# Differential attention's keys and queries prepared for both maps in one 128-row pass, with copies inside SBUF that put the halves in place

## The chip, the cores and the metric

The kernel runs on one core of one Trainium2 chip. The metric is the device time of one execution in microseconds. TensorE (PE) multiplies matrices, VectorE (DVE), ScalarE (ACT) and GpSimd (POOL) work elementwise on 128 rows (partitions) at a time, and SyncE (SP) issues all the DMAs of this kernel, one after the other in its queue. Each engine takes its instructions in a fixed order.

## The reference

One streaming-encoder layer over 1024 prompt tokens and 32 sample tokens. The part that matters here is head group B, differential attention: four heads, two softmax maps each, 64 features a map.

```python
dq = proj[..., o3:o4].reshape(b, s, H_B, 2, D_HB)     # 4 heads, 2 maps, 64 features
dk = proj[..., o4:o5].reshape(b, s, H_B, 2, D_HB)
...
s = jnp.einsum('bqhmd,bkhmd->bhmqk', qb, k).astype(jnp.float32) * scale
s = s - slopes[None, :, None, None, None] * dist      # and a block-causal mask
p = jax.nn.softmax(s, axis=-1)
w = jnp.einsum('bhmqk,hm->bhqk', p, coef32)           # map 0 minus lambda times map 1
return jnp.einsum('bhqk,bkhd->bqhd', w, v)
```

The layer goes on with latent attention (eight heads), an output projection, a layer norm, a gated convolution network, a second norm and a gate.

## The kernel before

All tensors are f32, and a product of two of them is made from a high part (rounded to fp32r) and a low part (the rest), in three matmuls: high by high, high by low, low by high. The stages follow each other: projections of the input, differential attention, latent attention (from about 387 us), output projection, feed-forward network, gate.

`dk` and `dq` hold, for each differential head h, a tile `hd(dk, h)` of 128 rows: rows 0 to 63 are map 0's features, rows 64 to 127 map 1's. A score product has only 64 features, so the kernel stacks parts on the 128 rows of PE: a tile K with the high part of the keys in one half of its rows and their low part in the other, and two tiles Qh and Ql with the queries' high and low part repeated in both halves. Then one matmul with Qh and one with Ql (L554 and L555) make a score block with all its parts.

`prep_b(h)` makes K, Qh and Ql. It is a list of six steps, and map m has three of them: `keys(m)` rounds the map's 64 rows of keys (ACT, L484) and of queries (POOL, L119 by way of L485), `low(m, 0)` and `low(m, 512)` subtract the high part from the 64 rows, 512 columns at a time (POOL, L82), and the last issues one DMA (L495) that copies the queries' 64 rows, high and low, to the other half. The keys' low part is written straight into the other half by POOL. So a head takes, on POOL, two roundings of 64x1024 and eight subtractions of 64x512, on ACT two roundings of 64x1024, and two DMAs of 512 KB.

`UnitB(h, i)` is one block of 128 queries, i from 7 (1024 keys) down to 0 (128 keys). `front` makes the scores of each map into a PSUM tile `pd` (two of these exist), a softmax pass on DVE with the bias and the row's maximum (L524), an exponential on ACT (L558), then on DVE a reciprocal, a coefficient and the combination of the two maps (L562). `back` transposes the result (PE L571, ACT L572), `values` multiplies by the values (PE L582), and after every four blocks POOL takes a power (L589), DVE scales the rows (four L592), and PE transposes them (L599). Head 0's steps of `prep_b` run between the products that make the differential values (`tok_tile` with `out_dv`, three matmuls at L144 to L146 for each of eight parts) and the sample tokens' attention (`sb_...`, with the transposes L424 and the products L438 and L442, which hold one `pd` tile, and with the key rows that `dk_rows` copies on ACT at L359 and writes out at L360). The steps for head h+1 are hooked to the blocks of head h.

The order of each engine's instructions isn't the order in which the code is written: a scheduler with a timeline of its own sets it at build time, by when it takes the operands to be there. `paced` and `held` tell it what an instruction shall not come ahead of; they add no wait on the chip.

## Time and profile before

| | |
|---|---|
| median of three runs | 1571.83 us (1571.09 to 1573.90) |
| the profiled execution | 1573.72 us, of it 1571.6 us from its first to its last instruction |
| granted TensorE clock, mean | 0.99 of full speed |
| PE busy | 1502.3 us, 96% |
| DVE busy | 965.8 us, 61% |
| ACT busy | 714.3 us, 45% |
| POOL busy | 342.6 us, 22% |

Busy time is the time in which an engine had an instruction in hand. The shares are means over all stages; what a change is worth is read in its own stage, here from 195 to 387 us.

### The profile page before, as it was taken

The numbers are of one execution on the slowest core, as the hardware profiler recorded it, in microseconds if no ns is written. First come the engines' busy times: TensorE is split into PE (matmuls) and PEld (weight loads), VectorE is DVE, ScalarE is ACT, GpSimd is POOL, SyncE is SP. The second block draws the span as 40 slices with busy tenths as digits, with TensorE's granted clock in tenths as the row PEclk, the third lists the DMA queues.
The fourth block names the chain that finished last, engine by engine and source line by source line (L and its number), as shares of the span: only waits on it lengthen the run. The fifth ranks groups of instructions, "written<-read, shape, count | busy, mean of one in ns | idle before, by whom it ended". The sixth has DMA issues, their size and how long they took to land.

```text
span 1571.6 us, 25325 instructions
## 1 busy us (share of the span) xinstructions
PE 1502.3 (96%) x9787; PEld 1361.5 (87%) x9787; DVE 965.8 (61%) x1944; ACT 714.3 (45%) x1754; POOL 342.6 (22%) x394
## 2 busy tenths in 40 slices
PE   7999998888989999989999999999989999998998
PEld 7999987768878789879999999999978787876887
DVE  4113336785767757598677777777788524279332
ACT  4223346777777765056455555555552302122111
POOL 0002034542454320001001111111120000049311
PEclk9999999999999999999999999999999999999999
DMA  6113251121110215132222222222265524130111
GB/s 208 48 48 89 71 168 48 28 69 37 25 49 15 65 48 202 41 101 56 74 82 82 82 82 68 69 72 81 88 225 164 160 50 123 68 113 28 41 44 44
DMA packets 125868, 127.89 MB, mean 81 GB/s; under 512 B 14701, under 2 KB 105461, under 8 KB 125493
## 3 DMA queue, kind: packets, MB, share of 16 engines
q1 hardware_dynamic: 125749, 126.28, 26.4%
q8 instruction: 77, 1.26, 0.3%
q14 instruction: 42, 0.34, 0.1%
HBM read 93.83 MB, written 26.07 MB: 76 GB/s over the span
## 4 chain that ended last, share of the span: by engine, by line
PE 80%; DVE 9%; ACT 6%; DMA 2%; issue 2%; POOL 1%; SPq 0%; DVEq 0%; ACTq 0%; POOLq 0%
PE pm L144 13%; PE pm L146 13%; PE pm L145 13%; PE pd L1227 5%; PE pd L1225 5%; PE pd L1226 5%; PE pm L1225 4%; PE pm L1227 4%; PE pm L1226 4%; DVE h L82 3%; ACT h L85 2%; PE pm L822 2%; DVE h L524 1%; PE pm L152 1%; PE pm L153 1%
## 5 line engine op out<-in xcount | busy, mean ns | idle before, releaser
L144 PE MATMUL pm<-h,h 128*128 128x512 f32 (+4 forms) x1076 | 366.8, 341 | 6.9 <-DVE h L82 3.4
L146 PE MATMUL pm<-h,h 128*128 128x512 f32 (+4 forms) x1076 | 363.2, 338 | 0.5 <-DVE h L82 0.5
L145 PE MATMUL pm<-h,h 128*128 128x512 f32 (+4 forms) x1076 | 362.9, 337 | 0.0
L144 PEld LDWEIGHTS pm<-h,h 128*128 128x128 f32 x1076 | 204.5, 190 | 28.9 <-DVE h L82 4.2
L146 PEld LDWEIGHTS pm<-h,h 128*128 128x128 f32 x1076 | 203.3, 189 | 20.0 <-DVE h L82 0.9
L145 PEld LDWEIGHTS pm<-h,h 128*128 128x128 f32 x1076 | 203.5, 189 | 19.1 <-issue 0.5
L85 ACT CAST h<-t 128x1024 fp32r<-128x1024 f32 (+6 forms) x91 | 82.0, 912 | 211.3 <-PE pm L146 94.3
L82 DVE TENSOR_TENSOR h<-t,h 128x1024 fp32r<-128x1024 f32 (+6 forms) x81 | 88.9, 1107 | 100.4 <-ACT h L85 100.3
L82 DVE TENSOR_TENSOR h<-pm,h 128x256 fp32r<-128x256 f32 (+7 forms) x221 | 101.8, 485 | 47.5 <-ACT h L85 45.4
L1238 DVE SCALAR_TENSOR_TENSOR h<-h,cp,h 128x1058 f32<-128x1058 f32 x88 | 115.8, 1318 | 21.5 <-ACT h L1246 20.7
L1212 ACT COPY h<-pd 128x256 f32<-128x256 f32 (+1 forms) x258 | 56.2, 270 | 124.5 <-PE pd L1227 124.4
L85 ACT CAST h<-pm 128x256 fp32r<-128x256 f32 (+7 forms) x221 | 88.2, 426 | 44.2 <-PE pm L803 19.6
L1225 PE MATMUL pm<-h,s 128*128 128x264 f32 x360 | 102.5, 287 | 4.6 <-ACT h L1212 4.6
L82 DVE TENSOR_TENSOR h<-h,h 128x512 fp32r<-128x512 f32 (+4 forms) x166 | 101.0, 640 | 2.1 <-ACT h L85 2.1
L1226 PE MATMUL pm<-h,s 128*128 128x264 f32 x360 | 101.8, 285 | 0.0
L1227 PE MATMUL pm<-h,s 128*128 128x264 f32 x360 | 99.9, 286 | 0.0
L1227 PE MATMUL pd<-h,s 128*128 128x264 f32 x344 | 98.0, 285 | 0.0
L1225 PE MATMUL pd<-h,s 128*128 128x264 f32 x344 | 97.8, 284 | 0.0
L1226 PE MATMUL pd<-h,s 128*128 128x264 f32 x344 | 97.7, 284 | 0.0
L1387 DVE TENSOR_TENSOR h<-pm,h 128x512 f32<-128x512 f32 x48 | 32.9, 684 | 75.4 <-PE pm L146 75.4
L82 DVE TENSOR_TENSOR s<-h,s 128x512 fp32r<-128x512 f32 (+1 forms) x96 | 60.5, 642 | 29.3 <-ACT s L85 29.1
L178 POOL TENSOR_TENSOR sm<-sm,neghalf 128x1 f32<-128x1 f32 (+1 forms) x37 | 22.7, 614 | 253.9 <-DVE sm L177 249.0
(326 smaller groups left out, 3733.6 us busy)
## 6 DMA issues: line engine op xcount, KB each, us to landing
h<-in_w_up SPq DMA_DIRECT2D x44, 512.0 KB, 5.0
zd<-h SPq DMA_DIRECT2D x22, 529.0 KB, 4.1
t<-zd SPq DMA_DIRECT2D x24, 384.0 KB, 3.6
t<-in_w_down SPq DMA_DIRECT2D x16, 512.0 KB, 3.2
h<-in_x_p SPq DMA_DIRECT2D x15, 512.0 KB, 5.7
t<-in_w_in SPq DMA_DIRECT2D x14, 512.0 KB, 4.0
h<-h SPq DMA_DIRECT2D x8, 512.0 KB, 5.0
t<-in_w_o SPq DMA_DIRECT2D x8, 512.0 KB, 3.5
```

The lines of the kernel that those rows point to most:

```text
L82: return eng.tensor_tensor(out, x, y, ALU.subtract)
L85: c = ACT.copy(hi, src)
L144: PE.matmul(ps, sh, mh, start=(i == 0), stop=False)
L145: PE.matmul(ps, sh, ml, start=False, stop=False)
L146: PE.matmul(ps, sl, mh, start=False, stop=(i == last))
L822: PE.matmul(po[:, c : c + 256], vt[k // 4][:, k % 4, h % 4], pts[k // 4][:, hl, k % 4], start=(k == 0 and hl == 0), stop=(k == kt - 1 and ...
L1212: ACT.copy(x, y)
L1225: PE.matmul(ps[:, :BW], w[:, 0, k], c[:, k, 0], start=first and k == 0, stop=False, skip_group_check=True)
L1226: PE.matmul(ps[:, :BW], w[:, 0, k], c[:, k, 1], start=False, stop=False, skip_group_check=True)
L1227: PE.matmul(ps[:, :BW], w[:, 1, k], c[:, k, 0], start=False, stop=k == 3, skip_group_check=True)
L1238: DVE.scalar_tensor_tensor(z[:, j], U[:, j, i : i + T], cp[:, i, m + j * NF : m + j * NF + 1], z[:, j], ALU.mult, ALU.add)
L1387: DVE.tensor_tensor(d, ps[:n], d, ALU.add)
```

## The change

The six steps of `prep_b` become five. `begin` takes all three tile pairs at once (K for both maps, q0 and q1) and rounds all 128 rows of keys (one ACT instruction) and of queries (one POOL instruction) into map 0's tiles. `low_k` subtracts on 128 rows, two instructions of 512 columns, into the tile that will be map 1's Qh (t), and issues three DMAs of 256 KB: map 1's high keys to map 1's K, and the two halves of t to where map 1's and map 0's low keys belong. `low_q` subtracts on 128 rows, two instructions, and issues three DMAs of 512 KB: map 1's queries from q0's rows 64 to 127 into both halves of q1, and map 0's queries from q0's rows 0 to 63 over q0's rows 64 to 127. The last writes where the two ahead of it read, and these write where the keys' DMAs read.

```diff
@@ -475,26 +475,35 @@
                 load(bm[0][:, :1024], a["c_dist"])
             paced(scale(POOL, bm[h][:, :1024], bm[max(h - 1, 0)][:, :1024], 0.25 if h else -2.0))
 
-        def keys(m):
-            r, q = m * 64, 64 - m * 64
-            if m == 0:
-                V["k"] = pair()
-            K, Q = V["k"][:, m], pair()
-            Qh, Ql = Q[:, 0], Q[:, 1]
-            paced(ACT.copy(K[r : r + 64, :1024], hd(dk, h)[r : r + 64, :1024]))
-            paced(scale(POOL, Qh[r : r + 64, :1024], hd(dq, h)[r : r + 64, :1024], 1.0))
-            kq[h, m] = (K, Qh, Ql, Q)
-
-        def low(m, c):
-            r, q = m * 64, 64 - m * 64
-            K, Qh, Ql, Q = kq[h, m]
+        def begin():
+
+            V["k"], q0, q1 = pair(), pair(), pair()
+            K = V["k"]
+            kq[h, 0], kq[h, 1] = (K[:, 0], q0[:, 0], q0[:, 1], q0), (K[:, 1], q1[:, 0], q1[:, 1], q1)
+            paced(ACT.copy(K[:, 0, :1024], hd(dk, h)[:, :1024]))
+            paced(scale(POOL, q0[:, 0, :1024], hd(dq, h)[:, :1024], 1.0))
+
+        def low_k(c):
+            K, t = kq[h, 0][0], kq[h, 1][1]
             cs = slice(c, c + 512)
-            paced(sub(POOL, Ql[r : r + 64, cs], hd(dq, h)[r : r + 64, cs], f(Qh[r : r + 64, cs])))
-            paced(sub(POOL, K[q : q + 64, cs], hd(dk, h)[r : r + 64, cs], f(K[r : r + 64, cs])))
+            paced(sub(POOL, t[:, cs], hd(dk, h)[:, cs], f(K[:, cs])))
             if c:
-                SP.dma_start(f(Q[q : q + 64, :, :1024]), f(Q[r : r + 64, :, :1024]))
-
-        return [lambda: (bias(), keys(0)), lambda: low(0, 0), lambda: low(0, 512), lambda: keys(1), lambda: low(1, 0), lambda: low(1, 512)]
+
+                K1 = kq[h, 1][0]
+                SP.dma_start(f(K1[64:128, :1024]), f(K[64:128, :1024]))
+                SP.dma_start(f(K1[0:64, :1024]), f(t[64:128, :1024]))
+                SP.dma_start(f(K[64:128, :1024]), f(t[0:64, :1024]))
+
+        def low_q(c):
+            q0, q1 = kq[h, 0][3], kq[h, 1][3]
+            cs = slice(c, c + 512)
+            paced(sub(POOL, q0[:, 1, cs], hd(dq, h)[:, cs], f(q0[:, 0, cs])))
+            if c:
+                SP.dma_start(f(q1[0:64, :, :1024]), f(q0[64:128, :, :1024]))
+                SP.dma_start(f(q1[64:128, :, :1024]), f(q0[64:128, :, :1024]))
+                SP.dma_start(f(q0[64:128, :, :1024]), f(q0[0:64, :, :1024]))
+
+        return [lambda: (bias(), begin()), lambda: low_k(0), lambda: low_k(512), lambda: low_q(0), lambda: low_q(512)]
 
     steps += prep_b(0)
```

The scheduler moves instructions in answer. Lines behind the change stand nine lines further down in the new file (L563 and L564 are L554 and L555, L580 is L571, L591 is L582, L608 is L599, L519 is L510). First PE, from the sample tokens' products to the first differential scores; `pd_2284` is the sample tokens' accumulator, `pd_2445` and `pd_2452` the scores of head 0's first block (maps 0 and 1) before. The difference:

```order
 L424 MATMUL pm_2264<-ident,s_2095 128x128
 L438 MATMUL pd_2284<-t_2285,s_1650 128x512
-L554 MATMUL pd_2445<-h_2358,h_2359 128x512
-L555 MATMUL pd_2445<-h_2358,h_2359 128x512
-L554 MATMUL pd_2445<-h_2358,h_2359 128x512
-L555 MATMUL pd_2445<-h_2358,h_2359 128x512
 L424 MATMUL pm_2268<-ident,s_2095 128x128
 L438 MATMUL pd_2284<-t_2285,s_1650 128x512
```

And where they stand in the changed kernel, as `pd_2443` and `pd_2450`, behind all the products of the differential values:

```order
L146 MATMUL pm_2395<-h_2005,h_89 128x256
L442 MATMUL pd_2284<-rows_s,ptl 128x512
L563 MATMUL pd_2443<-h_2358,h_2359 128x512
L564 MATMUL pd_2443<-h_2358,h_2359 128x512
L563 MATMUL pd_2443<-h_2358,h_2359 128x512
L564 MATMUL pd_2443<-h_2358,h_2359 128x512
L563 MATMUL pd_2450<-h_2358,h_2360 128x512
```

Both maps' scores of the first block have gone from ahead of the four products of the values to behind them; before, the second block's scores stood at that place.

The second place is PE where head 0 ends. Before, `pd_2710` and `pd_2717` are head 1's first scores:

```order
L571 MATMUL pm_2702<-ident,h_2609 128x128 x3
L554 MATMUL pd_2710<-h_2464,h_2465 128x512
L555 MATMUL pd_2710<-h_2464,h_2465 128x512
L554 MATMUL pd_2710<-h_2464,h_2465 128x512
L555 MATMUL pd_2710<-h_2464,h_2465 128x512
L582 MATMUL pm_2695<-h_1597,s_2701 128x128 x3
L554 MATMUL pd_2717<-h_2464,h_2569 128x512
```

In the changed kernel they are `pd_2706` and `pd_2713`:

```order
L580 MATMUL pm_2698<-ident,h_2608 128x128 x3
L608 MATMUL pm_2734<-ident,sm_2664 128x128
L591 MATMUL pm_2691<-h_1597,s_2697 128x128 x3
L580 MATMUL pm_2760<-ident,h_2640 128x128 x2
L608 MATMUL pm_2734<-ident,sm_2664 128x128 x3
L580 MATMUL pm_2788<-ident,h_2676 128x128
L563 MATMUL pd_2706<-h_2462,h_2463 128x512
```

Head 1's first scores now stand behind head 0's last transposes, its last block (L580 of `h_2676`) among them; the same holds where heads 1 and 2 meet.

The third place is SP's queue during head 0's preparation. `h_2358` is K, `h_2359` q0, `h_2360` q1 (first t):

```order
L360 DMA out_dk_p<-sm_2132 128x512
L494 DMA h_2358<-h_2360 64x1024
L495 DMA h_2358<-h_2360 64x1024
L519 DMA out_dv_p<-h_1597 128x512
L503 DMA h_2360<-h_2359 64x2x1024
L360 DMA out_dk_p<-sm_2167 128x512
L360 DMA out_dk_p<-sm_2175 128x512
L502 DMA h_2360<-h_2359 64x2x1024
L519 DMA out_dv_p<-h_1597 128x512
L360 DMA out_dk_p<-sm_2210 128x512
L360 DMA out_dk_s<-sm_2218 32x512
L504 DMA h_2359<-h_2359 64x2x1024
```

Between the same writes of key rows (L360) there was one copy (L495) before; now there are five, of which L503, L502 and L504 wait for copies ahead of them.

## Rows read from the trace of the kernel before

**Rows 1.** The page of the profile: the span, the busy time of PE, and the chain that ended last by engine.

```profile
span 1571.6 us, 25325 instructions
...
PE 1502.3 (96%) x9787; PEld 1361.5 (87%) x9787; DVE 965.8 (61%) x1944; ACT 714.3 (45%) x1754; POOL 342.6 (22%) x394
...
PE 80%; DVE 9%; ACT 6%; DMA 2%; issue 2%; POOL 1%; SPq 0%; DVEq 0%; ACTq 0%; POOLq 0%
```

**Rows 2.** Busy time by stretch. Columns: the stretch, its length, then each engine's busy us (instructions), the granted clock as a share of full speed, the DMA engines' share and GB/s.

```profile
core 0: us, PE busy (x) PEld busy (x) DVE busy (x) ACT busy (x) POOL busy (x), PEclk, DMA share, GB/s
223.00:244.00 21.00, 21.00 (x126) 16.24 (x125) 5.29 (x13) 5.97 (x14) 1.04 (x1) 1.00 0.30 103
244.00:265.80 21.80, 19.73 (x135) 16.78 (x134) 17.45 (x51) 18.16 (x54) 12.53 (x12) 1.00 0.26 61
265.80:292.60 26.80, 23.72 (x156) 20.66 (x154) 22.34 (x63) 21.75 (x60) 14.46 (x11) 0.94 0.10 21
292.60:325.60 33.00, 27.30 (x181) 23.79 (x181) 26.34 (x74) 24.31 (x72) 18.23 (x15) 0.95 0.27 60
325.60:350.00 24.40, 18.00 (x99) 13.82 (x98) 22.89 (x59) 19.34 (x52) 6.94 (x5) 0.92 0.21 52
350.00:387.00 37.00, 33.09 (x214) 30.02 (x213) 23.74 (x78) 25.87 (x87) 10.88 (x11) 0.91 0.16 40
387.00:860.00 473.00, 448.29 (x3177) 415.52 (x3176) 345.90 (x795) 275.87 (x701) 108.66 (x163) 0.99 0.23 70
```

**Rows 3.** Timeline of DVE, the first block of head 0 (128x1024) and the second (128x896). Columns: start us, duration us, engine, line, operation, tiles, shapes, count, and in brackets the idle time before it with what ended it.

```profile
228.83 1.22 DVE L524 CUSTOM_DVE_ANT_0 h<-pd,s 128x1024 f32<-128x1024 f32 x1 [0.49 <-PE pd L555]
...
231.88 1.28 DVE L562 SCALAR_TENSOR_TENSOR h<-h,sm 128x1024 f32<-128x1024 f32 x1
...
245.68 1.09 DVE L524 CUSTOM_DVE_ANT_0 h<-pd,s 128x896 f32<-128x896 f32 x1 [12.51 <-PE pd L555]
...
247.36 1.09 DVE L524 CUSTOM_DVE_ANT_0 h<-pd,s 128x896 f32<-128x896 f32 x1 [0.52 <-PE pd L555]
```

**Rows 4.** Timeline of PE, the score matmuls of the first block: the first and the last of map 0's four and of map 1's four.

```profile
223.34 0.80 PE L554 MATMUL pd<-h,h 128*128 128x512 f32 x1
...
224.44 0.39 PE L555 MATMUL pd<-h,h 128*128 128x512 f32 x1
...
227.61 0.48 PE L554 MATMUL pd<-h,h 128*128 128x512 f32 x1
...
228.40 0.40 PE L555 MATMUL pd<-h,h 128*128 128x512 f32 x1
```

**Rows 5.** The chain that ended last, in order of time, from 211 us: start us, duration us, what.

```profile
211.05 4.09 DMA out_dk_p<-sm
...
216.57 4.79 DMA out_dk_p<-sm
...
221.45 0.58 ACT sm L359
```

**Rows 6.** POOL's timeline (columns of rows 3): the rounding of map 1's queries of head 0, and the two powers L589 that fall into head 1's blocks.

```profile
209.53 1.05 POOL L119 TENSOR_SCALAR h<-h 64x1024 fp32r<-64x1024 f32 x1 [3.89 <-PE pm L146]
...
280.41 1.84 POOL L589 TENSOR_TENSOR sm<-sm,neghalf 128x4 f32<-128x4 f32 x1 [5.72 <-DVE sm L588]
...
292.20 1.01 POOL L589 TENSOR_TENSOR sm<-sm,neghalf 128x4 f32<-128x4 f32 x1 [2.38 <-DVE sm L588]
```

**Rows 7.** Groups of POOL by line and shape, 195 to 400 us (count | busy us, mean ns of one | idle before and what ended it).

```profile
L82 POOL TENSOR_TENSOR h<-h,h 64x512 fp32r<-64x512 f32 x32 | 41.1, 1290 | 24.1 <-ACT h L484 22.5
...
L82 POOL TENSOR_TENSOR h<-t,h 128x1024 fp32r<-128x1024 f32 x1 | 2.4, 2390 | 4.4 <-PE pd L663 4.4
```

**Rows 8.** A group of ACT by line and shape, 195 to 387 us, with the same columns.

```profile
L484 ACT CAST h<-h 64x1024 fp32r<-64x1024 f32 x8 | 8.3, 1044 | 0.5 <-PE pm L146 0.2 <-PE pm L145 0.2
```

**Rows 9.** Timeline of DVE: the combination of the two maps (L562) twice at 128x768 and twice at 128x512.

```profile
255.00 1.02 DVE L562 SCALAR_TENSOR_TENSOR h<-h,sm 128x768 f32<-128x768 f32 x1
...
261.26 1.58 DVE L562 SCALAR_TENSOR_TENSOR h<-h,sm 128x512 f32<-128x512 f32 x1
...
282.55 1.78 DVE L562 SCALAR_TENSOR_TENSOR h<-h,sm 128x768 f32<-128x768 f32 x1
...
289.99 0.75 DVE L562 SCALAR_TENSOR_TENSOR h<-h,sm 128x512 f32<-128x512 f32 x1
```

**Rows 10.** Timeline of DVE where head 0 ends and head 1 begins: the last L562 of head 0, the four scalings L592, the first block's softmax pass for map 1 of head 1.

```profile
266.49 0.63 DVE L562 SCALAR_TENSOR_TENSOR h<-h,sm 128x128 f32<-128x128 f32 x1
...
268.20 1.12 DVE L592 SCALAR_TENSOR_TENSOR sm<-pm,sm,g 128x128 f32<-128x128 f32 x4
...
269.24 1.22 DVE L524 CUSTOM_DVE_ANT_0 h<-pd,s 128x1024 f32<-128x1024 f32 x1
```

**Rows 11.** The chain that ended last, in order of time, where heads 1 and 2 meet and where heads 2 and 3 meet (columns of rows 5).

```profile
294.60 4.31 DMA h<-h
...
326.04 4.32 DMA h<-h
```

**Rows 12.** Timeline of DVE: the first block's softmax pass for map 1 of heads 2 and 3.

```profile
300.25 1.23 DVE L524 CUSTOM_DVE_ANT_0 h<-pd,s 128x1024 f32<-128x1024 f32 x1 [1.94 <-PE pd L555]
...
331.72 1.23 DVE L524 CUSTOM_DVE_ANT_0 h<-pd,s 128x1024 f32<-128x1024 f32 x1 [1.28 <-PE pd L555]
```

**Rows 13.** The page's DMA issues: the 512 KB copies inside SBUF (count, KB each, median us from issue to landing).

```profile
h<-h SPq DMA_DIRECT2D x8, 512.0 KB, 5.0
```

## The prediction

> **What bounds the kernel now.** I read the page first. The span is 1571.6 us, PE is busy for 96% of it, and PE makes up 80% of the chain that ended last [rows 1]. So time is won or lost where PE is not the bound, or where PE's own order is held up. The change touches 195 to 387 us, so the busy time by stretch comes next [rows 2]. Two regimes stand there. From 223 to 244 us PE is busy for all 21.0 us (the products of the differential values) while DVE does 5.3. From 244 to 350 us DVE does 17.45 of 21.8, 22.34 of 26.8, 26.34 of 33.0 and 22.89 of 24.4 us, and PE falls to 18.0 of 24.4. There the softmax chain (scores, row maximum on DVE, exponential, combination on DVE) sets the pace. From 387 us PE has 448 of 473 us again. POOL, whose work the change halves, has 12.5 to 18.2 us a head and is not a bound; it matters by what waits for it. The last views are the timelines of DVE and PE at the three places where the order changes.
>
> **What it removes.** A head has eight subtractions of 64x512 at 1.29 us; 128x1024 takes 2.39 us, so the cost goes by columns and 128x512 will take 1.2 to 1.3 us [rows 7]. Four instead of eight save 5 us of POOL a head, one rounding 1.05 more [rows 6], and ACT saves 1.04 us [rows 8]. None of it is on the path by itself: POOL and ACT have gaps in every stretch [rows 2]. What can be seen of it is on DVE. A combination of 128x768 takes 1.02 us and at another time 1.78, one of 128x512 takes 0.75 and 1.58 [rows 9]; the long ones lie where POOL subtracts. The Trainium skill, "SBUF — State Buffer", section "Who interferes with whom", says that a DVE instruction with two SBUF inputs and a GpSimd instruction that reads SBUF shut each other out for a whole instruction; the trace agrees, 1.58 against 0.75 us. Per head 0.8 to 2.3 us of DVE is lost so. Not all is won back, as half of the subtractions stay: 0.3 to 1.2 us a head.
>
> **Head 0's first block, the largest term.** Before, its scores ran at 223.34 and 227.61 us [rows 4], and its softmax ended at 231.88 + 1.28 = 233.16 us [rows 3], all of it beside the products that keep PE busy; then DVE was idle for 12.51 us until the second block. In the new order the scores come behind the last of these products, where the second block's stood. The chain of this block now stands in the open: one pass of 1.22 us for map 0, then 4.33 us from map 1's pass (228.83) to the end of the combination (233.16), 5.55 us together. The second block's two passes, back to back, take 2.2 us more and end at 245.68 + 5.55 + 2.2 = 253.4 us, against 247.36 + 1.09 = 248.45 us. That is **+5.0 us** (4.3 if map 1's scores come without a wait for the sample tokens' accumulator).
>
> **The products ahead of it.** PE gets back the scores' place there, 1.5 + 1.2 us by [rows 4], some 2.4 where matmuls overlap. Against that stands SP's queue. The tile t takes the slot that map 1's queries had, which was not free until 209.53 us [rows 6]; two subtractions end at 212.1, and copy L494 lands 4.1 to 4.8 us after its issue, as the writes at that time did [rows 5], at 216.7 us. L503 waits for it at the head of the queue, and behind L503 stand the writes of the key rows. These are on the path: written from 211.05 to 215.14, then from 216.57 to 221.36, and then ACT, with the sample tokens' transposes behind it, at 221.45 [rows 5]. The second of these writes moves by about 1.8 us, and 1.25 MB more of copies share the DMA engines: 1.5 to 4 us, I take 2.4. Both together: **0** (-1 to +2).
>
> **Head 0's other blocks.** DVE is idle for 4.35 of the 21.8 us [rows 2], of which 1.68 ahead of the second block and 0.52 between its maps [rows 3]; the other 2.15 us can take up a delay, and POOL's lighter load gives up to 1.1 (two stretched combinations) [rows 9]. I take **-1.5** (0 to -3).
>
> **Where head 0 ends.** Before, the last combination ended at 267.12 and map 1's first pass of head 1 at 270.46, 3.34 us later [rows 10]. In the new order head 1's scores stand behind head 0's last transposes and scaled rows: some 0.7 of the power (1.01 us in [rows 6]) beyond the combination, four scalings 1.12 us [rows 10], some 0.5 us for transposes (an estimate from the 0.24 us or so that a score matmul adds to PE), four score matmuls 1.2, two passes of 1.22. That is 5.9 us, **+2.5** (1.5 to 3.5).
>
> **Where heads 1 and 2, and 2 and 3, meet.** Here the old kernel paid for its own copies: the second power of the head held POOL, the last subtractions came behind it, a copy left at 294.60 and took 4.31 us, and DVE was idle for 1.94 us until map 1's scores; at head 3 the copy took 4.32 and DVE was idle for 1.28 [rows 11, 12]. In the new order POOL is done ahead of the second power, but three copies follow one another: t's halves, q0 to q1, q0 onto itself. The first power ends at 282.25 [rows 6]; three subtractions bring 286.1, t's halves (issued at 283.6 and 284.2) land by 288.5, the next two, together 1 MB, by 293.4 to 295, the last by 297.7 to 299.5, as one takes 4.3 alone and 5.0 in the median [rows 11, 13]. Map 0's scores and pass then put map 1's pass at 300.1 to 301.9 us, against 300.25 [rows 12]: +0.5 for head 2, and at head 3, where other DVE work fills the wait (22.89 of 24.4 us), -0.5. Together **0** (-3 to +4), and **-0.5** (0 to -2) for DVE's shorter combinations in these heads. The Trainium skill, "DMA: Bandwidth & Descriptors", section "Anatomy of one DMA", gives 2.0 us and 436 GB/s, an estimate of 3.2 us for 512 KB. The trace has 4.31. By the page the chain of copies would be some 3 us shorter, head 2 would start without it, and the whole sum would be some 1.3 us lower.
>
> **The handover.** A delay at 350 us meets a PE that is busy for 33.1 of 37 us [rows 2], with latent attention's first products in between; **-1** (0 to -3). From there PE's order is the old one and its 95% leaves no room to catch up.
>
> **The sum.** 5.0 + 0 - 1.5 + 2.5 + 0 - 0.5 - 1 = +4.5 us. Against the profiled execution, 1573.72, that is 1578.2; it stands 1.9 us above the median of the runs, so for the median I predict 1571.83 + 4.5 = **1576.3 us**. About 0.2%, 3.1 us, is what a measurement of this kernel can tell from no change.
>
> **Rivals.** *Faster, by POOL's relief.* Every head loses up to 2.3 us of DVE to POOL and heads 2 and 3 lose 1.94 and 1.28 us to their copy. If all of that comes back in three heads, -6.9 - 3.2, and the boundaries cost nothing, against +5.0, the time is 1571.83 - 5.1 = 1566.7 us. It decides if the last copy lands before DVE has finished the head before, about 296 us on the old clock. The rows' 4.3 us a copy speak against it, and so does PE's order at the end of head 0. The rule on the shared port named above would work for it. Chance 0.12.
>
> *The delay is taken up.* The block in the open costs its 5.0, but head 0's idle time gives 2.15, POOL 1.1, the handover 2, and the end of head 0 adds only 1.5: +1.3, 1573.1 us. For it: the scheduler has filled other gaps; against: DVE's share in every stretch. Chance 0.26.
>
> *The copies become the wait.* If two 512 KB copies at once take 6 us or more and each link 5.0 [rows 13], heads 2 and 3 begin 2.5 us later each, and head 0's queue costs its upper 2: 4.5 + 5 + 2 = +11.5, 1583.3 us. For it: the DMA engines are light there (0.10 to 0.27 in [rows 2]), which speaks against the first, not the second. Chance 0.10.
>
> **Chances and range.** The forecast itself has 0.52, with its own range 1575 to 1581. Slower by over 0.2%: 0.52 + 0.10 = 0.62; the same: 0.26; faster: 0.12. The range reaches from 1569.0, halfway between the faster rival's time and the median of before (the lower half of that rival lies outside), to 1583.0, the time of the third rival; what lies outside is some 0.07 below and 0.06 above, with as much again for what I have not thought of.
>
> **What would show it.** Right: DVE's first softmax pass at about 245 us or later and no idle stretch of 12 us ahead of it; map 1's pass of head 1 some 6 us later than 269.24; copies L504 of heads 2 and 3 that land within 2 us of map 0's scores; latent attention's first pass 3 to 6 us later. Wrong: a first pass of head 1 no later than 272, combinations of 128x768 all near 1.0 us, or a wait of more than 3 us for copies at each head.

## The result, and the profile after

The changed kernel is slower. The median of its four runs is 1587.03 us (1584.48 to 1591.21), that of the kernel before beside them 1571.46; the ratio is 1.0100, 95% interval 1.0087 to 1.0112. The forecast was slower, but 1576.3 us, in a range up to 1583.0. The traced execution after took 1584.82 us, the traced one before 1573.72: +11.1, and between the spans +11.4.

The page of the profile after, the lines that answer to [rows 1] and [rows 13]:

```profile
span 1583.0 us, 25336 instructions
...
PE 1507.7 (95%) x9787; PEld 1363.2 (86%) x9787; DVE 964.2 (61%) x1944; ACT 709.1 (45%) x1750; POOL 317.3 (20%) x374
...
PE 77%; DVE 7%; ACT 6%; DMA 4%; issue 3%; POOL 2%; SPq 1%; DVEq 0%; ACTq 0%; POOLq 0%
...
h<-h SPq DMA_DIRECT2D x12, 512.0 KB, 5.5
```

POOL has 25.3 us less to do, ACT 5.2 less, and the kernel is longer: on the chain that ended last DMA has gone from 2 to 4%, "issue" from 2 to 3%, POOL from 1 to 2%. Busy time by stretch, the same stretches and columns as [rows 2]:

```profile
223.00:244.00 21.00, 20.23 (x117) 15.06 (x116) 1.33 (x6) 2.18 (x9) 0.00 (x0) 0.94 0.48 148
244.00:265.80 21.80, 19.13 (x105) 14.90 (x103) 15.83 (x39) 15.47 (x39) 7.53 (x7) 0.92 0.42 97
265.80:292.60 26.80, 21.63 (x147) 18.14 (x145) 20.25 (x60) 19.66 (x59) 9.78 (x8) 1.00 0.20 41
292.60:325.60 33.00, 26.50 (x163) 22.52 (x163) 22.22 (x69) 21.40 (x64) 9.09 (x8) 0.90 0.35 74
325.60:350.00 24.40, 21.18 (x145) 17.79 (x145) 20.71 (x63) 19.23 (x56) 3.42 (x3) 1.00 0.51 113
350.00:387.00 37.00, 27.48 (x153) 23.68 (x152) 28.35 (x70) 27.82 (x84) 13.81 (x12) 0.86 0.22 57
387.00:860.00 473.00, 447.04 (x3155) 413.36 (x3156) 341.21 (x803) 273.69 (x705) 107.10 (x160) 0.99 0.21 66
```

The stretches are fixed times, and from head 0's second block on the same work lies 4 to 12 us later than in the rows of before; so a stretch is not the same work in both. DVE does less in every stretch up to 350 us, and PE no more in its place (apart from 325 to 350). The DMA engines' share has gone up in each of them and up to 387 us. From 387 us on the old picture holds. TensorE's granted clock is no longer 1.00 from 223 to 265 us; run 12 comes back to that.

**Head 0's first block.** DVE's timeline, which answers to [rows 3]:

```profile
246.51 1.22 DVE L533 CUSTOM_DVE_ANT_0 h<-pd,s 128x1024 f32<-128x1024 f32 x1 [17.69 <-PE pd L564]
...
247.73 1.22 DVE L533 CUSTOM_DVE_ANT_0 h<-pd,s 128x1024 f32<-128x1024 f32 x1
...
250.77 1.28 DVE L571 SCALAR_TENSOR_TENSOR h<-h,sm 128x1024 f32<-128x1024 f32 x1
...
252.98 1.09 DVE L533 CUSTOM_DVE_ANT_0 h<-pd,s 128x896 f32<-128x896 f32 x1
```

The idle time now stands ahead of the first block (17.69 us) and the second ends its passes at 254.07 against 248.45 us.

**Where head 0 ends**, which answers to [rows 10]:

```profile
270.89 0.35 DVE L571 SCALAR_TENSOR_TENSOR h<-h,sm 128x128 f32<-128x128 f32 x1
...
275.24 1.23 DVE L533 CUSTOM_DVE_ANT_0 h<-pd,s 128x1024 f32<-128x1024 f32 x1 [1.96 <-PE pd L564]
...
276.39 1.22 DVE L533 CUSTOM_DVE_ANT_0 h<-pd,s 128x1024 f32<-128x1024 f32 x1
```

Map 1's pass of head 1 starts at 276.39 against 269.24: +7.15 us.

**Where heads 1 and 2 meet.** The chain that ended last from 287 us, in order of time, which answers to [rows 11]; SP's lines are the copies' issues:

```profile
287.77 1.01 POOL sm L598
288.79 1.25 POOL h L82
...
290.60 4.14 DMA h<-h
...
294.82 0.62 SPq L502
...
295.49 6.44 DMA h<-h
...
301.99 4.34 DMA h<-h
...
306.47 0.47 PE pd L563
```

And DVE there and where heads 2 and 3 meet, which answers to [rows 12]:

```profile
307.67 1.22 DVE L533 CUSTOM_DVE_ANT_0 h<-pd,s 128x1024 f32<-128x1024 f32 x1 [4.77 <-PE pd L564]
...
309.26 1.23 DVE L533 CUSTOM_DVE_ANT_0 h<-pd,s 128x1024 f32<-128x1024 f32 x1 [0.37 <-PE pd L564]
...
341.13 1.22 DVE L533 CUSTOM_DVE_ANT_0 h<-pd,s 128x1024 f32<-128x1024 f32 x1 [1.32 <-PE pd L564]
...
342.61 1.22 DVE L533 CUSTOM_DVE_ANT_0 h<-pd,s 128x1024 f32<-128x1024 f32 x1
```

The whole chain is three copies deep, 4.14 + 6.44 + 4.34 us, and the scores follow the last landing by 0.14 us. At head 3 the same chain ends with

```profile
328.28 7.15 DMA h<-h
...
335.50 4.29 DMA h<-h
```

Map 1's pass starts 2.9 us behind the last landing at head 2 (309.26 - 306.33) and 2.8 at head 3 (342.61 - 339.79). Map 1's passes come 9.01 and 10.89 us later than before. Latent attention's first POOL instruction (L119 at 128x1024) is 11.68 us later, 400.04 against 388.36.

### The profile page after: what moved, and what is told of

The parts are those of the page before. It is cut to its first block, busy times and chain, and to the rows that moved or that the text cites. A ratio compares the mean times of both kernels' runs of the same rounds, so it can differ in the third digit from the quotient of the medians.

```text
span 1583.0 us, 25336 instructions
## 1 busy us (share of the span) xinstructions
PE 1507.7 (95%) x9787; PEld 1363.2 (86%) x9787; DVE 964.2 (61%) x1944; ACT 709.1 (45%) x1750; POOL 317.3 (20%) x374
## 4 chain that ended last, share of the span: by engine, by line
PE 77%; DVE 7%; ACT 6%; DMA 4%; issue 3%; POOL 2%; SPq 1%; DVEq 0%; ACTq 0%; POOLq 0%
PE pm L144 13%; PE pm L146 13%; PE pm L145 13%; PE pd L1234 5%; PE pd L1236 5%; PE pd L1235 5%; PE pm L1234 4%; PE pm L1235 4%; PE pm L1236 4%; ACT h L85 3%; DVE h L82 2%; DMA h<-h 2%; PE pm L831 2%; POOL h L82 1%; PE pm L152 1%
```

## The experiments

Theory A after reading the two traces: the time goes where the scheduler placed head 0's first block, and at the boundaries of the heads to the wait for the last copy. Rivals: the load of the copies on the DMA engines and SP's queue, or the order of PE at the boundaries by itself. All of the runs, in one table; times in us against the traced execution of before, read from the start times in each trace's timelines (the second block by the end of its last pass). The last two columns compare the medians of the runs made side by side, and count for the verdict: the traced execution of before lies some 2 us above the median of its kernel.

| | last product L442 | second block | map 1's pass, head 1 | head 2 | head 3 | latent attention | span | medians | ratio (95%) |
|---|---|---|---|---|---|---|---|---|---|
| before | 243.51 | 248.45 | 269.24 | 300.25 | 331.72 | 388.36 | 1571.6 | | |
| after | +0.6 | +5.6 | +7.2 | +9.0 | +10.9 | +11.7 | +11.4 | +15.6 | 1.0100 (1.0087-1.0112) |
| 1 head 0 old | -0.5 | -0.5 | +0.5 | +3.1 | +5.4 | +4.2 | +2.2 | +5.5 | 1.0037 (1.0026-1.0048) |
| 2 head 0 new | +0.8 | +6.5 | +9.1 | +9.6 | +9.8 | +11.4 | +15.4 | +15.8 | 1.0096 (1.0081-1.0111) |
| 3 order alone | -1.8 | +4.0 | +6.6 | +8.6 | +9.3 | +8.5 | +7.8 | +9.8 | 1.0057 (1.0039-1.0075) |
| 4 map 0 one hop | +2.7 | +2.7 | +3.5 | +3.9 | +6.2 | +5.9 | +6.2 | +6.3 | 1.0038 (1.0023-1.0053) |
| 5 phases earlier | +0.6 | +5.6 | +5.1 | +4.3 | +5.9 | +6.4 | +7.1 | +9.3 | 1.0055 (1.0039-1.0070) |
| 6 side by side | +4.2 | +4.2 | +5.3 | +4.2 | +5.0 | +6.1 | +4.7 | +6.8 | 1.0049 (1.0032-1.0066) |
| 7 high parts early | +2.9 | +2.9 | +1.8 | -1.0 | -3.1 | -0.6 | -0.9 | +1.2 | 1.0006 (0.9997-1.0016) |
| 8 keys alone | -3.4 | -3.4 | -0.9 | 0.0 | -0.6 | +1.0 | -0.8 | +3.1 | 1.0021 (1.0012-1.0031) |
| 9 head 0 old, rest as 7 | -1.2 | -1.2 | -2.3 | -4.8 | -7.3 | -1.8 | -4.1 | -2.5 | 0.9984 (0.9975-0.9993) |
| 10 head 0 keys, rest as 7 | -3.0 | -3.0 | -4.1 | -6.9 | -8.9 | -6.3 | -8.7 | -4.7 | 0.9964 (0.9952-0.9977) |
| 11 boundary order | -0.1 | -0.1 | +0.8 | +0.2 | -0.4 | +2.9 | +2.3 | +3.9 | 1.0025 (1.0015-1.0034) |
| 12 copies' load | +4.3 | +4.3 | +4.3 | +4.5 | +3.0 | +2.5 | +2.1 | +4.6 | 1.0022 (1.0013-1.0032) |
| 13 after again | +1.0 | +6.0 | +7.5 | +10.1 | +12.4 | +14.7 | +17.4 | +17.0 | 1.0099 (1.0081-1.0116) |

### 1 and 2: the change in some heads only

The steps of before for the heads that the condition names, those of the change for the others; run 2 has `if h != 0`:

```diff
+        if h == 0:
+            def keys(m):
...
+            return [lambda: (bias(), keys(0)), lambda: low(0, 0), lambda: low(0, 512), lambda: keys(1), lambda: low(1, 0), lambda: low(1, 512)]
         def begin():
```

> Head 0 is prepared per map as before, heads 1 to 3 for both maps at once as after. In PE's order the first block's scores are back in their early places, beside the products of the differential values, but head 1's first scores still stand behind the last transposes and scaled rows of head 0. Theory A (the places in PE's order set the cost, and head 0's first block is the largest part): the 5.6 us at the second block (end of its second pass 254.07 after, 248.45 before) go, the boundaries' 3.0, 1.9 and 0.4 and the handover's 2.3 stay, so +5 to +7.5 us against before. Theory B (the copies of heads 1 to 3 anchor each head's start, head 0 would only wait for them): +9 to +11. Theory C (it was head 0 alone): +2 or less.

> The other way round: head 0 for both maps at once, heads 1 to 3 per map. The first block's scores stand behind the last product; head 1's first scores stand again ahead of head 0's last values. Theory A: the 5.6 us at the second block, less what head 0 gives back (1.5), less nothing at the boundaries: +3 to +5.5 us against before. Theory B: within 1.5 us of before, as head 1's old preparation gives the delay back. Theory C: +9 to +11.

With head 0 prepared in the old way the second block's delay is gone, and the boundaries cost 1.0, 2.6 and 2.3 us: +5.5 of the medians, within theory A's range. Its parts are not theory A's: the last boundary costs 2.3 where it had 0.4, and from head 3 to latent attention 1.2 us come back where it had 2.3 more to lose. Run 2 came out beyond every expectation. Its heads 2 and 3 add only 0.5 and 0.2 us, so what the boundaries cost in the changed kernel belongs to the new preparation of those heads; but head 0 new alone already puts head 1 at +9.1, 1.9 more than in the full change, and this execution lost another 4.0 us behind latent attention's first pass. Up to head 1, run 2 is run 3 below with products that end 2.5 us later: +0.8, +6.5 and +9.1 against -1.8, +4.0 and +6.6. The 4.0 us go with the granted clock, which is 0.91 at 480 to 500 and at 540 to 560 us in this trace and 1.00 there in that of run 3. The two runs do not add up to the whole (5.5 + 15.8 against 15.6), and why head 0 alone comes to as much in the medians is not settled beyond these places.

### 3: the order alone, with before's own preparation

```diff
-    PE.matmul(po[:, :512], V["ptl"], dv_s, start=False, stop=True)
+    V["last"] = PE.matmul(po[:, :512], V["ptl"], dv_s, start=False, stop=True)
...
-    PE.matmul(ps[:, c : c + w], Qh[:, i * 128 : (i + 1) * 128], K[:, c : c + w], start=True, stop=False)
+    sc = PE.matmul(ps[:, c : c + w], Qh[:, i * 128 : (i + 1) * 128], K[:, c : c + w], start=True, stop=False)
+    if h == 0 and i == 7:
+        behind(sc, V["last"])
```

> The kernel before, with one edge more: the first score product of head 0's first block may not stand ahead of the last product of the sample tokens' sum. Nothing is computed or copied differently, so this prices the order alone. Theory A: as with the new preparation in head 0, +3.5 to +6 us, first softmax pass at 245 us or later. Rival (the new copies' load on the DMA engines and SP's queue is the cost, the order is not): within 1 us of before.

DVE's timeline of this run at the first block:

```profile
244.16 1.22 DVE L524 CUSTOM_DVE_ANT_0 h<-pd,s 128x1024 f32<-128x1024 f32 x1 [16.65 <-PE pd L557]
...
248.41 2.00 DVE L564 SCALAR_TENSOR_TENSOR h<-h,sm 128x1024 f32<-128x1024 f32 x1
```

No byte more is copied, and the kernel is 9.8 us slower, 3.8 beyond what theory A expected (the first pass, at 244.16, is 0.8 ahead of its sign). The order is thus a cost by itself, and the rival, by which it is none, falls. From the last product to the second block it costs 5.7 us (4.0 + 1.8), to head 1's pass 8.4; the changed kernel pays 5.0 and 6.5 there. Most of the difference stands in the combinations of DVE (the first, at 128x1024, takes 2.00 us here and 1.28 in the changed kernel). Groups of DVE by line and shape from 244 to 300 us, this run, and then the changed kernel (count | busy us, mean ns of one | idle before):

```profile
L564 DVE SCALAR_TENSOR_TENSOR h<-h,sm 128x896 f32<-128x896 f32 x2 | 3.2, 1600 | 0.1
L564 DVE SCALAR_TENSOR_TENSOR h<-h,sm 128x768 f32<-128x768 f32 x2 | 2.4, 1207 | 0.0
L564 DVE SCALAR_TENSOR_TENSOR h<-h,sm 128x512 f32<-128x512 f32 x2 | 1.9, 950 | 0.0
```

```profile
L571 DVE SCALAR_TENSOR_TENSOR h<-h,sm 128x896 f32<-128x896 f32 x2 | 2.3, 1152 | 0.1
L571 DVE SCALAR_TENSOR_TENSOR h<-h,sm 128x768 f32<-128x768 f32 x2 | 2.0, 1006 | 0.0
L571 DVE SCALAR_TENSOR_TENSOR h<-h,sm 128x512 f32<-128x512 f32 x2 | 1.5, 746 | 0.0
```

With half as many subtractions on POOL no combination of these shapes is stretched here. This agrees with the rule of the Trainium skill, "SBUF — State Buffer", section "Who interferes with whom", 0.75 us against a mean of 0.95 at 128x512. The scheduler answers the one added edge with other changes of order further on, so the 2.0 us at the boundary of heads 1 and 2 in this run are not explained by the first block alone, and the 9.8 us are the price of the first block's place together with this answer.

### 4, 5 and 6: the chain of copies

Run 4, the copies of `low_q`, whose subtraction now writes q1 (t lies in q0):

```diff
-                SP.dma_start(f(q1[0:64, :, :1024]), f(q0[64:128, :, :1024]))
-                SP.dma_start(f(q1[64:128, :, :1024]), f(q0[64:128, :, :1024]))
-                SP.dma_start(f(q0[64:128, :, :1024]), f(q0[0:64, :, :1024]))
+                SP.dma_start(f(q0[0:64, :, :1024]), f(q1[0:64, :, :1024]))
+                SP.dma_start(f(q0[64:128, :, :1024]), f(q1[0:64, :, :1024]))
+                SP.dma_start(f(q1[0:64, :, :1024]), f(q1[64:128, :, :1024]))
```

Run 5, the list of steps:

```diff
-        return [lambda: (bias(), begin()), lambda: low_k(0), lambda: low_k(512), lambda: low_q(0), lambda: low_q(512)]
+        return [lambda: (bias(), begin()), lambda: (low_k(0), low_k(512)), lambda: (low_q(0), low_q(512))]
```

Run 6, the copies out of a pair x of their own, into which the rounding and the subtraction write:

```diff
+                for d, r in ((q0[0:64], 0), (q0[64:128], 0), (q1[0:64], 64), (q1[64:128], 64)):
+                    SP.dma_start(f(d[:, :, :1024]), f(x[r : r + 64, :, :1024]))
```

> As after, but the query rows of both maps are made in the tile that map 1 uses: map 0's two halves then come by two copies side by side, one hop behind the last subtraction, and only map 1's second half takes the second hop (t takes the tile of map 0). Work and bytes are the same. Head 0's first block stands in its early places again, the boundaries still behind the transposes. Theory A: the 5.6 us at the second block go, but for a wait of 0 to 3 us of PE for the copies at 222 us; the boundaries lose one hop of 4.3 us where they wait for it (4.1 us of PE in two waits): +2 to +6 us against before. Rival (the load of the copies costs, whatever their order): +9 to +11.

> As after, but the preparation is handed out in three steps in place of five (both halves of a subtraction in one step), so that in heads 1 to 3 the last subtraction and with it the chain of copies starts some two blocks earlier. Work, copies and their chain are the same, head 0's first block still stands behind the products. Theory A1 (what the boundaries cost is that the last copy lands 5.5 to 8 us after the head's last combination): the copies of heads 2 and 3 land 4 to 6 us earlier, map 1's pass of these heads stands +7 to +8 us against before in place of +9.0 and +10.9, and the whole is +11 to +13 us in place of +15.6 of the median. Rival A2 (the order at the boundaries stays behind the transposes, however early the copies land): map 1's passes stay at +9 and +10.9, whole +14 to +17.

> As after, but the query rows of both maps are made in a tile of their own and four copies (two for each map) take them to their places, none of them behind another; t has its own half of that head's key pair's neighbour as before. Bytes copied per head grow from 2.25 to 2.75 MB. Head 0's first block stands in its early places. If a chain of two hops is the cost, the four land within some 8.6 us of the last subtraction in place of 13.8, and the boundaries are worth 2 to 3 us less each: +2 to +4 us against before. If the bytes are the cost (two copies of 512 KB at once took 6.4 us where one took 4.3), four at once take 12 us or more, map 1's passes of heads 2 and 3 stay at +3 to +6, and the whole is +5 to +9 us.

Run 5 changes least: same work, same chain, same place of the first block, only the start earlier (and the scheduler, which sees that, places the next head's scores forward). Its chain that ended last, at head 2:

```profile
290.75 6.87 DMA h<-h
297.68 4.33 DMA h<-h
```

and, at head 3, its last copy alone:

```profile
327.88 6.91 DMA h<-h
```

The last copy lands at 302.0 in place of 306.3 us and at 334.8 in place of 339.8; map 1's passes follow the landings again by 2.5 and 2.8 us, and move from +9.0 and +10.9 to +4.3 and +5.9. The medians move from +15.6 to +9.3, about what run 3 costs. So the wait for the late copies is the second part of the loss, and A2 falls; the gain is larger than A1 expected (+7 to +8 for the passes, +11 to +13 for the whole). What is left at the boundary of heads 2 and 3, 1.7 us, has its last copy issued behind six loads of latent attention's weights in SP's queue (L112, 321.27 to 327.78 us), and it took 6.91 us in place of 4.3. Run 4 brings head 0's block back to its early place and is 6.3 us slower than before, 0.3 beyond what was expected: the key rows' write beside the copies takes 6.47 us, the products end 2.7 later, and the third boundary still costs 2.2 (a pair of copies still takes 7.04 us, at head 2). In run 6 no copy waits for another. Four of them were issued from 322.29 us on at head 3, and the last took

```profile
325.63 9.78 DMA h<-h
```

so from the first issue to the last landing the four took 13.1 us, beside loads of weights, and the products ended 4.2 us late. That is the rival's landing (12 us or more, against 8.6), and +6.8 of the medians is its range: the bytes count. They count at another place than in run 4, though. The boundaries together add 0.8 us in run 6 and 3.5 in run 4, the products' end 4.2 and 2.7.

### 7: the high parts sent early

Rows made in q1 and three steps, as in runs 4 and 5, t in a pair of its own, and in `begin`, `low_k` and `low_q`:

```diff
+            paced(ACT.copy(K[64:128, 1, :1024], hd(dk, h)[64:128, :1024]))
...
+            for r in (0, 64):
+                SP.dma_start(f(q0[r : r + 64, 0, :1024]), f(q1[0:64, 0, :1024]))
...
+                SP.dma_start(f(K[64:128, :1024]), f(t[0:64, :1024]))
                 SP.dma_start(f(K1[0:64, :1024]), f(t[64:128, :1024]))
...
+                for r in (0, 64):
+                    SP.dma_start(f(q0[r : r + 64, 1, :1024]), f(q1[0:64, 1, :1024]))
+                SP.dma_start(f(q1[0:64, :, :1024]), f(q1[64:128, :, :1024]))
```

> The version that the first runs point to: rows of both maps made at once in map 1's tile, map 0's two copies of the high part sent off right behind the rounding, so that behind the last subtraction only the low part (2 x 256 KB) is left for map 0, and map 1's second half after that; the key rows of map 1 rounded in their own place by a second short instruction of ACT, the low parts of the keys one hop each from a tile of their own; three steps in place of five. Theory A (places and the chain behind the last subtraction are the cost, POOL's shorter work is a gain of 1 to 2 us a head): head 0's products as in the run with one hop, +1 to +2.7; boundaries 0 or below; whole -2 to +3 us against before. Rival (any copying of the halves costs, through the DMA engines and SP's queue): +6 us or more.

DVE's passes of map 1, heads 2 and 3:

```profile
299.29 1.23 DVE L536 CUSTOM_DVE_ANT_0 h<-pd,s 128x1024 f32<-128x1024 f32 x1 [1.18 <-PE pd L567]
...
328.61 1.21 DVE L536 CUSTOM_DVE_ANT_0 h<-pd,s 128x1024 f32<-128x1024 f32 x1
```

No copy stands any more on the chain that ended last there, and the boundaries give 1.1, 2.7 and 2.2 us. So the new preparation gives 1 to 3 us a head where no copy is waited for. What is lost is 2.9 us at head 0's products, just beyond the 1 to 2.7 expected, and 2.5 between head 3 and latent attention: in the medians the run can't be told from before.

### 8: the keys alone

`begin` and `low_k` as in the change, but for the queries, which go map by map as before:

```diff
-            paced(scale(POOL, q0[:, 0, :1024], hd(dq, h)[:, :1024], 1.0))
+            paced(scale(POOL, Q[r : r + 64, 0, :1024], hd(dq, h)[r : r + 64, :1024], 1.0))
...
-                SP.dma_start(f(q1[0:64, :, :1024]), f(q0[64:128, :, :1024]))
-                SP.dma_start(f(q1[64:128, :, :1024]), f(q0[64:128, :, :1024]))
-                SP.dma_start(f(q0[64:128, :, :1024]), f(q0[0:64, :, :1024]))
+                SP.dma_start(f(Q[q : q + 64, :, :1024]), f(Q[r : r + 64, :, :1024]))
```

> One part of the change alone: the keys of both maps at once with their three copies of 256 KB, the queries map by map as before (with one copy each, of 512 KB, one hop). Head 0's first block is in its early places; head 1's first scores stand ahead of the transposed results' neighbours as before, but behind the last transposes. Theory A (the two-hop chain of the query copies makes the boundaries): map 1's passes of heads 1 to 3 within +2 us of before, whole 0 to +3 us. Rival (the key rounding on 128 rows, which stands behind both exponentials of a head's first block, and the key copies delay the rest): passes +3 to +6, whole +4 to +8 us.

The passes stay within 0.9 us of before, as theory A had it, and the time, +3.1, is at the edge. But the products end 3.4 us earlier than before, which no theory had, and the boundaries give most of it back (2.6 and 0.8 lost, 0.6 won). Counted from the products' end the passes are 2.6 to 3.4 us later than before, near the rival's 3 to 6; this run doesn't decide between the two.

### 9 and 10: what the runs point to

Run 9 has the steps of before for head 0 and those of run 7 for the others; run 10 has those of run 8 for head 0:

```diff
+        if h == 0:
+            def begin():
...
+            return [lambda: (bias(), begin()), lambda: low_k(0), lambda: low_k(512), lambda: (low_q(0, 0), low_q(0, 512)), lambda: query(1), lambda: (low_q(1, 0), low_q(1, 512))]
```

> Head 0 prepared per map as before, heads 1 to 3 as in the run with the high parts early. If the parts add up, as theory A has it: products ahead of the first block -0.5, boundaries as in that run (-1.1, -2.7, -2.2): map 1's passes of heads 1, 2, 3 at about -1.6, -4.3 and -6.5 us against before, whole -3 to -6 us. If the gain of that run came from head 0's own preparation (POOL and ACT earlier free), heads 1 to 3 give nothing: within 1.5 us of before.

> As the run before it in this list, but head 0's keys are made for both maps at once and its queries per map (as in the run of the keys alone, where the products ended 3.4 us earlier than before). If the parts add up: passes of heads 1 to 3 at -4.5, -7 and -9.4 us, whole -5 to -9 us. If the 3.4 us were a lucky meeting of copies and writes of that one program: as the run before it, -3 to -6 us.

The parts add up in the heads: -2.3, -4.8, -7.3 and -4.1, -6.9, -8.9 us, 0.5 to 0.8 beyond the expected in run 9 and within 0.5 of it in run 10. Of the 7.3 run 9 keeps 1.8 at latent attention, of 8.9 run 10 keeps 6.3. Both beat the kernel before, by 0.16 and 0.36%, a little less than expected. The whole of run 10, -4.7, lies in the range of its rival too, but the products' early end is no luck of one program: it is there again, 3.0 us. The page of run 10:

```profile
span 1562.9 us, 25348 instructions
...
PE 82%; DVE 8%; ACT 6%; DMA 2%; issue 1%; POOL 1%; SPq 0%; DVEq 0%; ACTq 0%; POOLq 0%
```

### 11 and 12: the two rivals by themselves

Both are the kernel before with an addition. Run 11 (`lastT` is the last transpose L571, `sc` the first score matmul):

```diff
+        if n in (8, 16, 24):
+            while waiting:
+                turned.append(waiting.pop(0))
+                turned[-1].back()
+                while len(turned) > 1:
+                    turned.pop(0).values()
...
+                    if h and i == 7:
+                        behind(sc, UnitB.lastT)
```

Run 12:

```diff
+                if m:
+                    SP.dma_start(f(V["x"][0:64, :, :1024]), f(kq[h, 0][3][0:64, :, :1024]))
+                    SP.dma_start(f(V["x"][64:128, :, :1024]), f(Q[64:128, :, :1024]))
```

> The kernel before, with the first scores of heads 1 to 3 held behind the last transposes of the head before them in PE's order, as the changed kernel's order has them. Nothing is computed or copied differently, and no copy is late. If the order at the boundaries is what costs there, map 1's passes of heads 1, 2 and 3 are 2 to 3 us later at each boundary (+2.5, +5, +7) and the whole is +5 to +8 us. If it is the wait for the late copies, which the order only follows, the passes stay within 1 us at each boundary and the whole within +3 us.

> The kernel before, with two more copies of 512 KB a head into a tile that nobody reads, sent off behind the last copy of a head's preparation. The order on PE is that of before up to the last block of head 1. This prices the load of the change's copies on the DMA engines and on SP's queue alone. If the load counts: the products' end 1 to 3 us later than before, map 1's passes of heads 2 and 3 another 1 to 2 us each, whole +3 to +6 us. If only waits for a copy count: 0 to +1.5 us.

The order at the boundaries costs +0.9, -0.6 and -0.6 us there: it only follows the late copies. It does cost 3.3 us between head 3 and latent attention, and the whole, +3.9, lies between the two expectations. The load of two copies more a head costs 4.3 us at head 0's products, more than the 1 to 3 expected, and 0.2 and -1.6 us at the later boundaries, where 1 to 2 each were expected. The chain that ended last shows the key rows' writes that took 4.09 and 4.79 us in [rows 5]:

```profile
209.72 6.53 DMA out_dk_p<-sm
...
216.97 6.23 DMA out_dk_p<-sm
```

They take 2.44 + 1.44 = 3.9 us longer, but the first is issued 1.33 us earlier than before (209.72 against 211.05), and ACT's copy behind the second starts at 223.30 against 221.45: 1.9 us late. The rest of the 4.3, 2.4 us, comes behind it, on PE. PE had waited 3.32 us for that copy, 1.23 before, and then its granted clock stood at the lower of its two levels (1.2 in place of 2.4 GHz) for a part of the stretch. Columns of [rows 2], first before, then run 12:

```profile
222.00:228.00 6.00, 5.88 (x21) 3.19 (x22) 2.66 (x10) 2.96 (x13) 0.00 (x0) 1.00 0.27 94
222.00:228.00 6.00, 4.07 (x9) 2.48 (x10) 1.03 (x5) 1.69 (x7) 0.00 (x0) 0.57 0.28 98
```

In these 6 us the clock is 0.50 to 0.72 in the changed kernel (both traces) and in runs 2, 4, 5, 6, 7 and 12, in which the products end later than before, and 1.00 before and in runs 1, 3 and 8 to 11, in which they don't. The chain of the changed kernel shows what it does there:

```profile
223.12 1.71 PE pd L438 x2
...
226.32 5.72 DMA t<-in_cache_dv
```

The two products L438 take 0.86 us before; the second line is a load of the sample tokens' cached values, beside the copies. So this rival is real at one place, the products of head 0, by the waits of PE for DMAs and by the lower clock behind them.

### 13: the changed kernel once more

> The changed kernel itself, unaltered, for a second trace and more executions. Its first four executions lay at 1584.5, 1584.8, 1589.2 and 1591.2 us with a granted clock of 0.988, 0.986, 0.983 and 0.980; the traced one is the second fastest. If the slower ones differ by more stretches at the lower clock behind the heads (as in the traced execution of the run with head 0 new, 0.982, which lost 4.0 us behind latent attention's first pass and has stretches at 0.91 at 480 and 560 us), a trace at 0.983 or less shows the same map 1 passes (+7.2, +9.0, +10.9 within 1 us) and latent attention's first pass, and the loss behind them. If the copies vary, the passes of heads 2 and 3 move by 2 us or more. The median of all is expected at 1585 to 1588 us.

The traced execution was a long one, 1590.81 us; in all ten the kernel lies between 1584.48 and 1591.21, with a median of 1588.8, just above what was expected. Against the first trace of the same kernel it is 6.0 us longer in the span: 0.4 up to head 1, 0.7 and 0.4 at the two boundaries (DVE waited 5.58 and 2.62 us for the scores in place of 4.77 and 1.32), 1.5 between head 3 and latent attention, and 3.0 behind it. The passes of heads 2 and 3 move by 1.1 and 1.5 us, so neither expectation holds as it was put. What lengthens is mostly the clock. At head 2 the last copy lands at 306.6 in place of 306.3, and the scores behind it take 3.6 us in place of 2.8, more of them at the lower clock; at head 3 it is the copies, 7.54 in place of 7.15 us. From head 3's pass to latent attention the granted clock is 0.88 in place of 0.91 of some 58 us, about 1.9 us of clock for 1.5 lost. Behind latent attention's first pass the granted clock falls at two places where the first trace has none (second 13, first after; columns of [rows 2]):

```profile
420.00:430.00 10.00, 9.03 (x51) 8.00 (x50) 5.55 (x15) 5.55 (x13) 4.42 (x7) 0.83 0.00 0
480.00:500.00 20.00, 15.95 (x88) 13.89 (x88) 12.28 (x25) 15.84 (x42) 9.78 (x10) 0.91 0.13 27
```

```profile
420.00:430.00 10.00, 9.38 (x56) 8.31 (x57) 7.69 (x20) 8.20 (x20) 2.18 (x4) 1.00 0.00 0
480.00:500.00 20.00, 17.17 (x113) 15.46 (x114) 15.63 (x38) 15.43 (x37) 10.52 (x13) 1.00 0.07 15
```

10 x 0.17 + 20 x 0.09 = 3.5 us of clock, for 3.0 lost.

## Why the forecast was slower, and too small

In the order of its sum, for the traced execution (+11.4 of the span):

- **Products ahead, 0: held, +0.6, but by another way, so in part by luck.** Taking the scores away gives 1.75 us (run 3), the copies cost 2.4 beside them, as the sum had it. L503 did wait for L494 at the head of SP's queue, until 214.41 us. But the key rows' writes ended no later for it: the sample tokens' transposes behind them start at 222.02 us, 222.08 before. What cost the 2.4 is PE at the lower clock behind its wait, some 1.5 us, and for the rest the load of cached values beside the copies (both lines under run 12). The prediction put the cost on the key rows' writes and had no term for the clock.
- **First block in the open, +5.0: held to 0.1** (5.62 - 0.61). The first pass stands at 246.51, as foretold; the other sign, no idle 12 us ahead of it, was put wrongly, as the idle time only moves ahead of this pass.
- **Head 0's other blocks, -1.5, and its end, +2.5: held, -1.5 and +3.0.** The last combination is 4.12 us late, the pass of head 1 7.15. The power waited for the last sums on DVE and ended 0.9 us behind the last combination in place of 0.7, and the transposes took 0.75 in place of 0.5 us, which is the 0.5.
- **Boundaries of heads 1/2 and 2/3, 0, with -0.5 for DVE: this step failed, +3.7.** The mechanism, three copies in a chain ahead of the scores, was the right one, and the landing at head 2 was forecast rightly: 306.33 less the 7.15 of delay is 299.2 us, in the range 297.7 to 299.5. Wrong was what I took from it. I used the middle of the range, and 2.4 us from the landing to map 1's pass, which took 2.9: so +0.5 became +1.9. At head 3 I let other DVE work fill the wait, -0.5, where the pass again follows the last landing by 2.8 us. The pair of copies ahead of it took 7.15 us and was issued only at 327.6 and 328.3: t's halves had to leave the tile that it writes, and by the chain that ended last five loads of weights (L112) stood ahead of it in SP's queue, which the forecast did not count. That is +1.9 again. The shorter combinations, too, gave nothing that could be seen: what the shorter work gives, 1 to 3 us a head by run 7, ended here in the wait for the scores, 4.77 us at head 2. The same work begun earlier (run 5) gives -0.8 and +1.7.
- **The handover, -1: failed, +0.8** (2.3 in run 13). I took PE to be the bound from 350 to 387 us, as it did 33.1 of 37 us before, so that a part of the delay would vanish there. Busy time from head 3's pass to latent attention (columns of [rows 2]), before and after:

```profile
331.72:388.36 56.64, 47.76 (x292) 41.55 (x291) 42.15 (x121) 42.14 (x127) 16.11 (x14) 0.91 0.15 39
342.61:400.04 57.43, 46.80 (x285) 40.81 (x284) 43.15 (x119) 42.18 (x127) 17.25 (x15) 0.91 0.15 38
```

PE does much the same in both, at the same clock. But on the chain that ended last it makes up 27.7 of these 56.6 us before and 16.7 of 57.4 after, and ACT 10.9 and 23.1: the delay did not meet a bound on PE. From head 3's pass to latent attention, the runs whose heads end earlier than before (7 to 11) lose 1.6 to 5.5 us; of those that end later, some win back 0.2 to 1.2 and others lose 0.5 to 2.3. Run 11 says that the order at the boundaries counts for it; what it is beyond that stays open.
- **The rest, 0: -0.3.**

Together 0.6 + 5.0 + 1.5 + 3.7 + 0.8 - 0.3 = 11.3. The forecast for the traced execution, 1578.2, was 6.6 us too low, 4.2 of it at the boundaries and 1.8 at the handover. That the total of the other terms came out within 1 us is owed to the first block and the end of head 0, which were worked out from rows, and to luck at the products. The other 4.1 us of the miss are no step of the change: I took 1.9 off for the traced execution of before, which lay above its median, and the traced one of after lay 2.2 below its own. The two traces of the changed kernel differ by 6 us, and most of that goes with spells at the lower clock, 3.0 behind latent attention's first pass and some 2 ahead of it; copies that took longer are 0.4 at head 3. What brings these spells about is not settled. Two bounds of the range were also not what they were said to be: halfway between the faster rival and before is 1569.3, and the third rival's time 1583.3; the measured time lies above either upper bound.

Of the signs, *right* came the first pass at 246.51, head 1's pass at +7.15 and the copies L504 that land 0.14 us ahead of the scores; latent attention, +11.7 in place of +3 to +6, did not. Of those for *wrong* one came fully (the four combinations of 128x768 take 0.99 to 1.02 us, so DVE's relief was there) and one in part (a wait of over 3 us for the copies at head 2, not at head 3).

Of the rivals, *the copies become the wait* (+11.5) was the right one, with the forecast's own first block; its 2.5 a head was 1.9, its queue 0.6 in place of 2. Of its conditions the pair held (6.44 us and more), the link of 5.0 did not (4.14 and 4.34). That its sum meets the span's +11.4 is luck: it had -1 for the handover, which cost 0.8. The words against it, that the DMA engines are light there, were a mean over a stretch: two copies at once took 6.4 to 7.5 us. *Faster, by POOL's relief* was right that there is a gain and wrong on the copies, as run 10 shows, where they land in time. *The delay is taken up* failed at three places: head 0's blocks gave 1.5 in place of 3.25, its end added 3.0 in place of 1.5, and the handover gave nothing.

## What to carry to other kernels

A change that shortens an engine's work but adds hops between the work and its user has to be timed by the last landing, with copies that leave together priced together, and with what each of them overwrites; sending what is ready early and starting earlier is worth more than the instructions saved. Where a build-time scheduler orders the engines, look first for what it moves: here one block put behind other work, with what the scheduler moved in answer, cost 9.8 us without any copy. And a wait of PE can cost more than its length, where the granted clock falls behind it (run 12). One trace of each kernel is no median: when the effect is under 1%, leave room for the spread of the new kernel as well as of the old.

## What the runs showed of the hardware

- A copy of 512 KB inside SBUF takes 4.3 us alone (run 5 and the changed kernel, head 2), the second of two issued together 6.4 to 7.5 (the changed kernel, runs 5 and 13), and four issued within 3.3 us of each other 13.1 from the first issue to the last landing (run 6, head 3, beside loads). The writes of key rows to DRAM beside two more of them take 6.5 and 6.2 in place of 4.1 and 4.8 (run 12). The Trainium skill, "DMA: Bandwidth & Descriptors", section "Anatomy of one DMA", gives 2.0 us and 436 GB/s, for 1 MB an estimate of 4.4 us; that section measures another path of issue, and the trace's 6.44 decides.
- From 222 to 228 us the granted clock was 1.00 before, when PE had waited 1.23 us for the key rows, and 0.57 in run 12, when it had waited 3.32; at the lower level two products L438 took 1.71 in place of 0.86 us.
- The granted clock fell to 0.83 at 420 to 430 and to 0.91 at 480 to 500 us in one execution and not in another of the same kernel (run 13).
